# A mixer layer in split fp32: later splits in the first pair, branches one after the other, last chunks bank by bank

## The chip, the cores and the metric

The kernel runs on one core of a Trainium2 chip. Its time is the device time of one execution in microseconds (us); shown is the median of some runs, and for the trace one profiled execution. The core's engines work through queues of their own, in order: TensorE (PE: matrix products into eight PSUM banks; PEld is its weight load), VectorE (DVE), ScalarE (ACT), GpSimd (POOL) and SyncE (SP), which issues most transfers.

## The reference

One layer over 512 tokens of width 2048. All three branches read the same normalised input, each is gated and projected back to width 2048, and their sum goes through one output product:

```python
h = rms_norm(x, norm_g[l]);  proj = h @ w_in[l]          # 2048 -> 13312, split into 13 parts
ya = (short_conv_mixer(a_b, a_c, a_x, conv_w[l]) * silu(a_z)) @ w_branch_a[l]
yb = (chunk_band_attention(q, k, v, ...) * silu(b_z)) @ w_branch_b[l]     # 8 heads of 128
mkv = rms_norm(mem, mem_norm_g[l]) @ w_mem_kv[l]         # 256 memory tokens; mk gets a norm per head
ym = (memory_attention(mq, mk, mv, ...) * silu(m_z)) @ w_branch_m[l]      # 4 heads
merged = sigmoid(g_a + b0) * ya + sigmoid(g_b + b1) * yb + sigmoid(g_m + b2) * ym
x = x + merged @ w_out[l]
```

## The kernel before

All products but the memory's are done in split precision: an fp32 operand is cut into a rounded part `hi` (a cast on ScalarE) and the rest `lo` (a subtraction on VectorE), and three matmuls (hi hi, hi lo, lo hi) stand for one (`split`, `products`, lines 182 to 205).

The wide products go in pairs of 512 columns (`pair`, line 235) by Strassen's scheme: tokens and rows, and columns, are halved, and seven products in the order P1, P5, P6, P3, P7, P2, P4 take the place of eight. Each has four chunks (256 rows of the halved weight, two banks, 12 matmuls), so a pair is 28 steps. A chunk needs its weight block or a difference of two (`raw`, one subtraction on VectorE) split into `whi` and `wlo`. The left operands are blocks of the tokens, A11, S1, S2, S4, S3, A12, A22 (line 233: which product takes which), built once by `Blocks` from four quarters: s1, s2, s4 and s3 are the sums and differences, and a name such as S4 is the split of one, each in two halves (0 and 1) of four rows each. `H` are the blocks of the normalised input, `M` those of the merged branches. A pair ends each product with an evacuation on VectorE (P1 on ScalarE).

The order is written out: a list of steps, each with loads (issued 6 steps ahead), the subtractions, the split of the weights of two steps later, the matmuls, what follows them (`post`), what a table puts at that step (`at_step`), what was put off by some steps (`after`) and tasks taken from a list with a budget per step (`run_steps`, line 123). Each engine keeps that order.

The steps: 16 for memory's keys and values (`kv_steps`, fp32 without a split, meanwhile x is normalised and turned), then the pairs q, k, v, cx, bz, mqz, az, six pairs of gates (beside them the attention's heads), then the branches' products (`branch`, line 798: slabs of four banks and 24 matmuls a step, two steps for a and m, four for b), which add into `mg`, and at last two output pairs o0 and o1 (`out_pair`). The turn of `mg` into the blocks of M is `m_turn`. Memory's head norm is `heads_out` with the name mk: squares on ScalarE, `rstd_of` (line 158: v, a power on GpSimd, then t and r on VectorE), a scaling and a turn. The tiles of the 512-wide intermediate results come from one pool of nine cells (`cel`), gates and x among them; split weights from three buffers each (`wst`).

Of the kernel before, what the change touches and what calls it, by code (L numbers as in the profile page):

```python
# [14 lines left out]
ALU = mybir.AluOpType  # L15
# [13 lines left out]
KB = 2  # L29
# [36 lines left out]
def trunk_layer(ctx: ExitStack, tc, x, mem, gx, gm, w_in, w_kv, bg, cw, hg, relz, w_a, w_b, w_m, w_o, out):  # L66
# [50 lines left out]
    def at_step(i, fn):  # L117
        at.setdefault(i, []).append(fn)
# [78 lines left out]
    def products(banks, w, acts, first, last, cont=False):  # L197

        whi, wlo = w
        for kk in range(KB):  # L200
            for t, ps in enumerate(banks):
                hi, lo = acts(kk, t)
                for i, (l, r) in enumerate(((hi, whi), (hi, wlo), (lo, whi))):
                    PE.matmul(ps, l, r[:, kk, :], start=first and kk == 0 and i == 0,
                              stop=last and kk == KB - 1 and i == 2, skip_group_check=cont)
# [26 lines left out]
    ORDER = ("P1", "P5", "P6", "P3", "P7", "P2", "P4")  # L232
    LEFT = {"P1": "A11", "P5": "S1", "P6": "S2", "P3": "S4", "P7": "S3", "P2": "A12", "P4": "A22"}

    def pair(name, left, w, done, bias=None):


        n = NK // 2 // KB
# [8 lines left out]
        def sub(dst, a, b, c):  # L247
            return lambda: DVE.tensor_tensor(raw[dst, c], raw[a, c], raw[b, c], op=ALU.subtract)
# [69 lines left out]
        for c in range(n):  # L318
            steps[s0 + c].loads.append(loader("11", 0, 0, c))
            steps[s0 + 1 + c].loads.append(loader("12", 0, 1, c))  # L320
            steps[s0 + 7 + c].loads.append(loader("22", 1, 1, c))
            steps[s0 + 19 + c].loads.append(loader("21", 1, 0, c))
            steps[s0 + c].adds.append(sub("11", "12", "11", c))
            steps[s0 + 5 + c].adds.append(sub("11", "22", "11", c))
            steps[s0 + (10, 12, 14, 16)[c]].adds.append(sub("12", "22", "12", c))
            steps[s0 + (20, 21, 22, 24)[c]].adds.append(sub("21", "21", "11", c))
        if bias is not None:
            def load_bias():
                st8["bias"] = bias()
            at_step(s0 - 2, load_bias)  # L330
# [74 lines left out]
    def kv_steps():  # L405
        st = {"ps": {}}
        for c in range(NK // KB):
            for half in range(2):
                def do_load(c=c, half=half):
                    st["raw", c, half] = load(w_kv[c * KB * P:(c + 1) * KB * P, half * S:(half + 1) * S], f"kv{half}_{c}")  # L410

                def mm(c=c, half=half):
                    if c == 0:
                        st["ps"][half] = [bank(f"ps_kv{half}_{t}") for t in range(NMT)]
                    for k in range(c * KB, (c + 1) * KB):
                        for t, ps in enumerate(st["ps"][half]):
                            PE.matmul(ps, mT[k // 8][:, k % 8, t * P:(t + 1) * P], st["raw", c, half][:, k % KB, :],
                                      start=k == 0, stop=k == NK - 1)

                s = Step(mm)  # L420
                s.loads.append(do_load)
                if c == NK // KB - 1:
                    def post(half=half):
                        cells = []
                        for t in range(NMT):
                            kv = cell(f"kv{half}_{t}")
                            ACT.mul(kv, st["ps"][half][t], rm[t])
                            cells.append(kv)
# [22 lines left out]
    class Blocks:  # L451


        def __init__(self, pre, slots, place):
            self.pre, self.slots, self.place, self.at, self.part = pre, slots, place, {}, {}

        def f(self, key, i):
            if key == (1, 1):
# [18 lines left out]
        def do(self, what, i):  # L477
            if what == "s1":
                self.combine("S12", (0, 1), (1, 1), ALU.add, i)
            elif what == "s2":  # L480
                self.combine("S12", "S12", (0, 0), ALU.subtract, i)
            elif what == "s4":
                self.combine("S4", (1, 0), "S12", ALU.subtract, i)
            elif what == "s3":
                self.combine((0, 1), (0, 0), (0, 1), ALU.subtract, i)
            else:
                key = {"A11": (0, 0), "S1": "S12", "S2": "S12", "S4": "S4", "S3": (0, 1), "A12": (1, 0), "A22": (1, 1)}
                self.split(what, i, key[what])

        def left(self, b):  # L490
# [23 lines left out]
        at_step(b + 2, lambda t=t: [x_turn(t, 2), x_turn(t, 3)])  # L514
    for i in range(2):
        for n, what in ((5 + i, "A11"), (7 + i, "A12"), (9, "s1"), (9, "s3"), (10, "S3"), (11, "S1"), (12, "s2"),
                        (12, "s4"), (13 + i, "S4"), (15 + i, "S2"), (17 + i, "A22")):
            at_step(n, lambda i=i, what=what: H.do(what, i))

    def w_pair(src, c0, c1=None):  # L520
# [277 lines left out]
    def branch(br, n, src, nk, names, first, end):  # L798
# [14 lines left out]
        def done(t, ps):  # L813
# [7 lines left out]
            if end is not None:  # L821
# [94 lines left out]
```

## Time and profile before

| what | us |
|---|---|
| median of three runs | 1515.0 (1514.83 to 1516.69) |
| the profiled execution | 1515.63, its span 1513.8 |
| TensorE busy | 1486.6, 98% of the span |
| VectorE busy | 1148.2, 76% |
| ScalarE busy | 706.7, 47% |
| granted TensorE clock, mean | 0.999 |

The span goes from the first to the last instruction of the trace. Busy shares are means over stages. Matmuls overlap their neighbours, so a single one shows 0.39 us where 48 in a row take 10.88. In a row of the timeline the brackets hold how long the engine was idle before, and what ended that.

### The profile page before, as it was taken

How to read it: one execution, taken by the hardware profiler on the slowest of the kernel's cores; microseconds unless marked ns; L12 is line 12 of the kernel's file. 1: busy time of each engine (PE TensorE's matmuls, PEld its weight loads, DVE VectorE, ACT ScalarE, POOL GpSimd, SP SyncE). 2: the span in 40 equal slices, each digit the busy share in tenths (PEclk: the TensorE clock that was granted, in tenths of full speed). 3: DMA queues.
4: the chain of work that ended last, by engine and by line, in shares of the span. 5: the costliest groups of instructions: out<-in, count | busy, mean ns of one | idle time of the engine just before them, and what ended most of it. 6: DMA issues, size and time to landing. Idle time of an engine off the chain costs nothing.

```text
span 1513.8 us, 17882 instructions
## 1 busy us (share of the span) xinstructions
PE 1486.6 (98%) x6696; PEld 1201.1 (79%) x6696; DVE 1148.2 (76%) x1393; ACT 706.7 (47%) x1102; POOL 22.0 (1%) x23
## 2 busy tenths in 40 slices
PE   8989999999999999999999999999999999998998
PEld 4468888788888888888888888888887888886786
DVE  3887778777888878887777778787887545579987
ACT  3565667543444465444444444444445333445442
POOL 0000000000000000000000000000000000000000
PEclk9999999999999999999999999999999999999999
DMA  9524354363326253625446362544735656510724
GB/s 325 190 70 141 135 171 143 92 223 111 119 91 208 70 195 88 201 94 206 134 156 220 106 227 88 186 141 133 254 133 203 207 183 195 201 43 21 256 78 132
DMA packets 139046, 233.45 MB, mean 154 GB/s; under 512 B 9808, under 2 KB 35408, under 8 KB 138320
## 3 DMA queue, kind: packets, MB, share of 16 engines
q1 hardware_dynamic: 130320, 215.54, 43.2%
q10 hardware_dynamic: 8640, 16.78, 3.4%
q8 instruction: 52, 0.85, 0.2%
q14 instruction: 34, 0.28, 0.1%
HBM read 198.73 MB, written 36.17 MB: 155 GB/s over the span
## 4 chain that ended last, share of the span: by engine, by line
PE 85%; DVE 9%; ACT 2%; issue 1%; DMA 1%; POOL 1%; SPq 0%; DVEq 0%; POOLq 0%; ACTq 0%
PE ps_wb L48 6%; PE psY_gb L48 4%; PE psY_ga L48 4%; PE psY_gm L48 3%; PE psY_o L48 3%; PE psZ_gm L48 3%; PE psZ_gb L48 3%; PE ps_wa L48 3%; PE ps_wm L48 3%; PE psZ_ga L48 3%; PE psY_k L48 2%; PE psY_cx L48 2%; PE psY_mqz L48 2%; PE psY_bz L48 2%; PE psY_q L48 2%; PE psY_az L48 2%
## 5 line engine op out<-in xcount | busy, mean ns | idle before, releaser
L48 ACT CAST whi_o_P<-raw_o 128x1024 fp32r<-128x1024 f32 x56 | 58.7, 1053 | 85.7 <-DVE raw_o L48 21.0
L48 DVE TENSOR_TENSOR wlo_gb_P<-raw_gb,whi_gb_P 128x1024 fp32r<-128x1024 f32 x56 | 68.1, 1222 | 31.4 <-ACT whi_gb_P L48 31.3
L48 DVE TENSOR_TENSOR wlo_ga_P<-raw_ga,whi_ga_P 128x1024 fp32r<-128x1024 f32 x56 | 68.2, 1223 | 31.0 <-ACT whi_ga_P L48 30.6
L48 DVE TENSOR_TENSOR wlo_gm_P<-raw_gm,whi_gm_P 128x1024 fp32r<-128x1024 f32 x56 | 68.5, 1223 | 22.8 <-ACT whi_gm_P L48 22.8
L48 DVE TENSOR_TENSOR wlo_o_P<-raw_o,whi_o_P 128x1024 fp32r<-128x1024 f32 x56 | 68.3, 1222 | 20.1 <-ACT whi_o_P L48 15.7
L48 ACT ACTIVATE p<-p,nm 128x128 f32<-128x128 f32 (+3 forms) x32 | 18.0, 564 | 108.4 <-DVE nm L48 100.9
L48 ACT CAST whi_gm_P<-raw_gm 128x1024 fp32r<-128x1024 f32 x56 | 58.8, 1051 | 20.4 <-PE psV_gm L48 5.2
L48 ACT CAST whi_ga_P<-raw_ga 128x1024 fp32r<-128x1024 f32 x56 | 58.1, 1049 | 10.8 <-PE psY_az L48 2.8
L48 ACT CAST whi_gb_P<-raw_gb 128x1024 fp32r<-128x1024 f32 x56 | 58.4, 1049 | 6.9 <-PE psY_gb L48 2.3
L48 ACT COPY p<-ptp 128x256 f32<-128x256 f32 (+3 forms) x48 | 19.6, 409 | 88.3 <-PE ptp L48 88.3
L48 PE MATMUL ps_kv<-raw_kv,mT 128*128 128x512 f32 x128 | 58.7, 612 | 0.3 <-DMA raw_kv<-in_w_kv 0.3
L48 PE MATMUL ps_wb<-whi_wb,yb_hi 128*128 128x512 f32 x128 | 49.8, 389 | 0.0
L48 PE MATMUL ps_wb<-whi_wb,yb_lo 128*128 128x512 f32 x128 | 49.8, 389 | 0.0
L48 PE MATMUL ps_wb<-wlo_wb,yb_hi 128*128 128x512 f32 x128 | 49.8, 389 | 0.0
L48 ACT CAST whi_cx_P<-raw_cx 128x1024 fp32r<-128x1024 f32 x28 | 29.6, 1056 | 42.9 <-PE psY_cx L48 13.2
L48 DVE TENSOR_TENSOR wlo_cx_P<-raw_cx,whi_cx_P 128x1024 fp32r<-128x1024 f32 x28 | 34.3, 1224 | 17.6 <-ACT whi_cx_P L48 15.9
L48 PEld LDWEIGHTS ps_kv<-raw_kv,mT 128*128 128x128 f32 x128 | 24.5, 197 | 28.4 <-issue 27.9
L48 DVE TENSOR_TENSOR wlo_mqz_P<-raw_mqz,whi_mqz_P 128x1024 fp32r<-128x1024 f32 x28 | 34.3, 1223 | 14.2 <-ACT whi_mqz_P L48 12.7
L48 DVE TENSOR_TENSOR wlo_v_P<-raw_v,whi_v_P 128x1024 fp32r<-128x1024 f32 x28 | 34.1, 1222 | 14.0 <-ACT whi_v_P L48 13.8
L48 ACT CAST whi_mqz_P<-raw_mqz 128x1024 fp32r<-128x1024 f32 x28 | 29.4, 1051 | 31.4 <-PE psZ_mqz L48 10.0
L48 ACT CAST whi_bz_P<-raw_bz 128x1024 fp32r<-128x1024 f32 x28 | 29.5, 1054 | 30.8 <-PE psZ_bz L48 7.7
L48 DVE TENSOR_TENSOR wlo_q_P<-raw_q,whi_q_P 128x1024 fp32r<-128x1024 f32 x28 | 34.2, 1223 | 12.5 <-ACT whi_q_P L48 12.3
(661 smaller groups left out, 4675.3 us busy)
## 6 DMA issues: line engine op xcount, KB each, us to landing
raw_ga<-in_w_in SPq DMA_DIRECT2D x32, 512.0 KB, 4.6
raw_gb<-in_w_in SPq DMA_DIRECT2D x32, 512.0 KB, 5.3
raw_gm<-in_w_in SPq DMA_DIRECT2D x32, 512.0 KB, 5.1
raw_o<-in_w_o SPq DMA_DIRECT2D x32, 512.0 KB, 6.8
raw_kv<-in_w_kv SPq DMA_DIRECT2D x16, 512.0 KB, 8.0
raw_q<-in_w_in SPq DMA_DIRECT2D x16, 512.0 KB, 4.4
raw_k<-in_w_in SPq DMA_DIRECT2D x16, 512.0 KB, 4.7
raw_v<-in_w_in SPq DMA_DIRECT2D x16, 512.0 KB, 4.5
```

The source lines that it names most:

```text
L48: ins = getattr(self.engine, op)(*args, **kwargs)
```

## The change

Four things:

- The first pair. The splits of the tokens' blocks S2, S4 and A22 move from steps 13 to 18 to steps 17 to 30 (the q pair begins at step 16), and mk's head norm begins seven steps later.
- The branches go one after the other, all four slabs of a, then of m, then of b, in place of a, m, b for each 512 columns. For that `M` uses other slots: s3 and S3 are done before the output pair instead of in it, and s1, s2, s4, S1, S2 are spread otherwise over its first steps.
- In the last chunk of every product (`last`) the matmuls go bank by bank, all of bank 0's before bank 1's, in place of row block by row block.
- In the output pairs x is added into the cells that the last product will be added to, at step 25 (`add_last`), in place of after it; and the last tile of all is stored in two halves, one issued by SyncE and one by ScalarE.

```diff
 def products(banks, w, acts, first, last, cont=False):
-        for kk in range(KB):
-            for t, ps in enumerate(banks):
+        nt = len(banks)
+        for j in range(KB * nt):
+            kk, t = (j % KB, j // KB) if last else (j // nt, j % nt)
...
 def pair(name, left, w, done, bias=None, addend=None):
+        def add_last():
+            for t, e in enumerate(addend()):
+                DVE.tensor_tensor(cs["a"][t], cs["a"][t], e, op=ALU.add)
+        if addend is not None:
+            at_step(s0 + 25, add_last)
...
 kv_steps
-                            heads_out("mk", cells, 0, hg_sb[:, 3:4], lambda t: mk_d[:, :, t * P:(t + 1) * P])
+                            after(7, lambda: heads_out("mk", cells, 0, hg_sb[:, 3:4], ...))
...
 for i in range(2):       # H, the tokens' blocks: step, what
-                        (12, "s4"), (13 + i, "S4"), (15 + i, "S2"), (17 + i, "A22")):
+                        (12, "s4"), (17 + 2 * i, "S2"), (21 + 2 * i, "S4"), (27 + 3 * i, "A22")):
...
-    M = Blocks("m", {..., "S4": (6, 7), "S3": (0, 13), "A12": (11, 1), "A22": (10, 12)}, {...})
+    M = Blocks("m", {..., "S4": (0, 1), "S3": (6, 7), "A12": (13, 10), "A22": (11, 12)}, {..., "S3": 10, ...})
...
     for n in range(4):
         branch("a", n, w_a, 4, ("ya",), True, None)
+    for n in range(4):
         branch("m", n, w_m, HM, ("ym",), False, None)
+    for n in range(4):
         branch("b", n, w_b, HB, ("yb0", "yb1"), False, m_turn)
...
-                       (7, "S4", 0), (8, "S4", 1), (10, "s3", 0), (10, "s3", 1), (11, "S3", 0), (12, "S3", 1),
+    for n, what, i in ((-7, "A11", 0), (-6, "A11", 1), (-5, "s3", 0), (-5, "s3", 1), (-4, "S3", 0), (-4, "S3", 1),
...
 out_pair, done
+                if (half, t0) != (0, 2):
+                    xr = xs.pop((half, t0 + k))
+                    DVE.tensor_tensor(c, c, xr, op=ALU.add)
+                if i == 1 and half == 0 and t0 == 2 and k == 1:
+                    for eng, j in ((SP, 0), (ACT, 1)):
+                        eng.dma_start(out[ts, n0 + j * MEM:n0 + (j + 1) * MEM], c[:, j * MEM:(j + 1) * MEM])
+                else:
+                    SP.dma_start(out[ts, n0:n0 + S], c)
```

VectorE's queue in the q pair before, from the second split of P1 to the fourth. `hS_lo<-hf_S_484` is a half of S2, `hS_lo<-hf_S_539` one of S4; `raw` is a subtraction of weight blocks, `wlo_q_P_n` the split of a product's chunk n, and v_mk to r_mk is the head norm:

```order
L48 TENSOR_TENSOR wlo_q_P_1_577<-raw_q_518,whi_q_P_1_576 128x1024
L48 TENSOR_TENSOR hS_lo<-hf_S_484,hS_hi 128x1024
L48 TENSOR_TENSOR raw_q_489<-raw_q_516,raw_q_489 128x1024
L48 TENSOR_TENSOR wlo_q_P_2_598<-raw_q_532,whi_q_P_2_597 128x1024
L48 TENSOR_TENSOR hS_lo<-hf_S_484,hS_hi 128x1024
L48 TENSOR_SCALAR v_mk_617<-ss_mk_571 128x8
L48 TENSOR_TENSOR t_mk_621<-r_mk_619 128x8
L48 TENSOR_TENSOR t_mk_621<-t_mk_621,v_mk_617 128x8
L48 TENSOR_SCALAR t_mk_621<-t_mk_621 128x8
L48 TENSOR_TENSOR r_mk_619<-r_mk_619,t_mk_621 128x8
L48 TENSOR_TENSOR raw_q_518<-raw_q_530,raw_q_518 128x1024
L48 TENSOR_TENSOR wlo_q_P_3_630<-raw_q_545,whi_q_P_3_629 128x1024
```

The same queue after, from the split of P6's chunk 1 to that of P6's chunk 2 (`pf` is the evacuation of the second product, P5):

```order
L48 TENSOR_TENSOR raw_q_532<-raw_q_640,raw_q_532 128x1024
L48 TENSOR_TENSOR wlo_q_P_1_734<-raw_q_518,whi_q_P_1_733 128x1024
L48 TENSOR_TENSOR pf_q_749<-psZ_q_671,pa_q_659 128x512
L48 TENSOR_TENSOR pf_q_750<-psZ_q_672,pa_q_660 128x512
L48 TENSOR_TENSOR hS_lo<-hf_S_539,hS_hi 128x1024
L48 TENSOR_SCALAR v_mk_755<-ss_mk_706 128x8
L48 TENSOR_TENSOR t_mk_759<-r_mk_757 128x8
L48 TENSOR_TENSOR t_mk_759<-t_mk_759,v_mk_755 128x8
L48 TENSOR_SCALAR t_mk_759<-t_mk_759 128x8
L48 TENSOR_TENSOR r_mk_757<-r_mk_757,t_mk_759 128x8
L48 TENSOR_TENSOR raw_q_545<-raw_q_665,raw_q_545 128x1024
L48 TENSOR_TENSOR wlo_q_P_2_766<-raw_q_532,whi_q_P_2_765 128x1024
```

The norm has moved from ahead of P1's last split to ahead of P6's third, six chunks later, where it now stands behind an evacuation and the last half of S4.

VectorE's queue at the start of the first output pair before, from the first subtraction for P5 (chunk 0's `raw`) on; `mf_S` are the sums s1, and `mS_lo` from them the two halves of S1:

```order
L48 TENSOR_TENSOR raw_o_110_10260<-raw_o_120_10300,raw_o_110_10260 128x1024
L48 TENSOR_TENSOR wlo_o_P_2_10490<-raw_o_112_10342,whi_o_P_2_10489 128x1024
L48 TENSOR_TENSOR raw_o_111_10302<-raw_o_121_10340,raw_o_111_10302 128x1024
L48 TENSOR_TENSOR wlo_o_P_3_10535<-raw_o_113_10386,whi_o_P_3_10534 128x1024
L48 TENSOR_TENSOR mf_S_10450<-mf_9544,mf_10213 128x1024
L48 TENSOR_TENSOR mS_lo<-mf_S_10450,mS_hi 128x1024 x2
L48 TENSOR_TENSOR raw_o_112_10342<-raw_o_122_10384,raw_o_112_10342 128x1024
L48 TENSOR_TENSOR wlo_o_P_0_10561<-raw_o_110_10260,whi_o_P_0_10560 128x1024
```

The same place after:

```order
L48 TENSOR_TENSOR raw_o_110_10237<-raw_o_120_10273,raw_o_110_10237 128x1024
L48 TENSOR_TENSOR wlo_o_P_2_10499<-raw_o_112_10318,whi_o_P_2_10498 128x1024
L48 TENSOR_TENSOR mS_lo<-mf_S_10425,mS_hi 128x1024
L48 TENSOR_TENSOR raw_o_111_10275<-raw_o_121_10316,raw_o_111_10275 128x1024
L48 TENSOR_TENSOR wlo_o_P_3_10548<-raw_o_113_10395,whi_o_P_3_10547 128x1024
L48 TENSOR_TENSOR mf_S_10425<-mf_10027,mf_10385 128x1024
L48 TENSOR_TENSOR mS_lo<-mf_S_10425,mS_hi 128x1024
L48 TENSOR_TENSOR raw_o_112_10318<-raw_o_122_10393,raw_o_112_10318 128x1024
L48 TENSOR_TENSOR wlo_o_P_0_10570<-raw_o_110_10237,whi_o_P_0_10569 128x1024
```

S1's halves, which stood side by side behind the second sum, now stand apart, the first two ops earlier and the second right behind its own sum; the first sum is done before this place in both.

Later in the same queue before, from P6's last split (not shown) to the fourth split of P3; `mf_9544<-mf_9531,mf_9544` are the two differences s3 and the `mS_lo` from mf_9544 the two halves of S3:

```order
L48 TENSOR_TENSOR raw_o_120_10300<-raw_o_220_10531,raw_o_120_10300 128x1024
L48 TENSOR_TENSOR wlo_o_P_0_10732<-raw_o_220_10531,whi_o_P_0_10731 128x1024
L48 TENSOR_TENSOR mf_9544<-mf_9531,mf_9544 128x1024 x2
L48 TENSOR_TENSOR wlo_o_P_1_10750<-raw_o_221_10557,whi_o_P_1_10749 128x1024
L48 TENSOR_TENSOR pe_o_10765<-psY_o_0_10694,pa_o_10595 128x512
L48 TENSOR_TENSOR pe_o_10766<-psY_o_1_10695,pa_o_10596 128x512
L48 TENSOR_TENSOR mS_lo<-mf_9544,mS_hi 128x1024
L48 TENSOR_TENSOR raw_o_121_10340<-raw_o_221_10557,raw_o_121_10340 128x1024
L48 TENSOR_TENSOR wlo_o_P_2_10775<-raw_o_222_10576,whi_o_P_2_10774 128x1024
L48 TENSOR_TENSOR mS_lo<-mf_9544,mS_hi 128x1024
L48 TENSOR_TENSOR wlo_o_P_3_10799<-raw_o_223_10601,whi_o_P_3_10798 128x1024
```

After, the same rows stand there without these four ops, which now come in the last branch slabs.

## Rows read from the trace of the kernel before

**Rows 1.** Waits of TensorE: us in total, times, longest.

```profile
PE psX_q L48 <- DVE wlo_q_P L48: 4.4, 3, 3.1
PE psY_o L48 <- DVE wlo_o_P L48: 4.1, 3, 1.5
PE psZ_o L48 <- DVE wlo_o_P L48: 3.8, 3, 1.5
PE ps_wa L48 <- DVE wlo_wa L48: 0.9, 1, 0.9
```

**Rows 2.** Stretches: length, busy PE, PEld, DVE, ACT, POOL; clock, DMA share, GB/s.

```profile
90.90:93.70 2.80, 2.77 (x7) 2.19 (x8) 2.80 (x3) 0.12 (x1) 0.00 (x0) 0.50 0.00 0
1357.00:1385.00 28.00, 22.96 (x96) 17.64 (x96) 28.00 (x26) 12.54 (x13) 0.00 (x0) 1.00 0.00 1
```

**Rows 3.** Timeline of TensorE, q pair: start, length, engine, operation, wait before.

```profile
76.09 0.79 PE L48 MATMUL psX_q<-whi_q_P,hA_hi 128*128 128x512 f32 x1
...
90.93 0.79 PE L48 MATMUL psX_q<-wlo_q_P,hA_hi 128*128 128x512 f32 x1 [3.07 <-DVE wlo_q_P L48]
...
94.86 0.40 PE L48 MATMUL psZ_q<-whi_q_P,hS_hi 128*128 128x512 f32 x1
```

**Rows 4.** Timeline of VectorE in the q pair's first product.

```profile
85.84 0.17 DVE L48 TENSOR_SCALAR v_mk<-ss_mk 128x8 f32<-128x8 f32 x1
87.83 0.17 DVE L48 TENSOR_TENSOR t_mk<-r_mk 128x8 f32<-128x8 f32 x1 [1.82 <-POOL r_mk L48]
...
88.53 1.22 DVE L48 TENSOR_TENSOR raw_q<-raw_q,raw_q 128x1024 f32<-128x1024 f32 x1
89.66 1.22 DVE L48 TENSOR_TENSOR wlo_q_P<-raw_q,whi_q_P 128x1024 fp32r<-128x1024 f32 x1
```

**Rows 5.** Timeline of ScalarE: the copies of the first product.

```profile
94.37 1.28 ACT L48 COPY pa_q<-psX_q 128x512 f32<-128x512 f32 x2 [3.35 <-PE psX_q L48]
```

**Rows 6.** Chain that ended last: the second output pair's first product.

```profile
1432.23 10.88 PE psX_o L48 x48
```

**Rows 7.** Timeline of TensorE, first output pair.

```profile
1344.12 0.39 PE L48 MATMUL psX_o<-whi_o_P,mA_hi 128*128 128x512 f32 x1
...
1379.66 0.50 PE L48 MATMUL psY_o<-wlo_o_P,mS_hi 128*128 128x512 f32 x1 [1.14 <-DVE wlo_o_P L48]
```

**Rows 8.** Timeline of VectorE, last branch slab and first output pair.

```profile
1339.96 1.23 DVE L48 TENSOR_TENSOR wlo_o_P<-raw_o,whi_o_P 128x1024 fp32r<-128x1024 f32 x1 [3.08 <-ACT whi_o_P L48]
1342.28 0.69 DVE L48 TENSOR_TENSOR g_b<-ps_wb,g_b 128x512 f32<-128x512 f32 x1 [1.09 <-PE ps_wb L48]
...
1347.59 1.22 DVE L48 TENSOR_TENSOR raw_o<-raw_o,raw_o 128x1024 f32<-128x1024 f32 x1
...
1352.14 1.22 DVE L48 TENSOR_TENSOR mf_S<-mf,mf 128x1024 f32<-128x1024 f32 x1
1353.27 2.43 DVE L48 TENSOR_TENSOR mS_lo<-mf_S,mS_hi 128x1024 fp32r<-128x1024 f32 x2
...
1384.06 2.36 DVE L48 TENSOR_TENSOR mf<-mf,mf 128x1024 f32<-128x1024 f32 x2
...
1388.66 1.22 DVE L48 TENSOR_TENSOR mS_lo<-mf,mS_hi 128x1024 fp32r<-128x1024 f32 x1
```

**Rows 9.** Timeline of ScalarE: the cast of the second half of S1.

```profile
1353.39 1.06 ACT L48 CAST mS_hi<-mf_S 128x1024 fp32r<-128x1024 f32 x1 [1.97 <-DVE mf_S L48]
```

**Rows 10.** Timeline of the end: VectorE, and SyncE's queue (SPq).

```profile
1507.75 1.37 DVE L48 TENSOR_TENSOR pa_o<-psY_o,pa_o 128x512 f32<-128x512 f32 x2 [4.61 <-PE psY_o L48]
1509.04 1.28 DVE L48 TENSOR_TENSOR pa_o<-pa_o,xr 128x512 f32<-128x512 f32 x2
1509.75 0.94 SPq L48 DMA_DIRECT2D out_y<-pa_o  x2
```

**Rows 11.** Issues of transfers: KB each, median us to landing.

```profile
g_a<-g_da SPq DMA_DIRECT2D x16, 256.0 KB, 7.2
...
out_y<-pa_o SPq DMA_DIRECT2D x4, 256.0 KB, 2.5
```

More of the change, by code (lines that the diff above doesn't have):

```diff
@@ L199, in products @@
         whi, wlo = w
-        for kk in range(KB):
-            for t, ps in enumerate(banks):
[L202 to L205, printed above, removed]
+        nt = len(banks)
+        for j in range(KB * nt):
+            kk, t = (j % KB, j // KB) if last else (j // nt, j % nt)
+            hi, lo = acts(kk, t)
+            for i, (l, r) in enumerate(((hi, whi), (hi, wlo), (lo, whi))):
+                PE.matmul(banks[t], l, r[:, kk, :], start=first and kk == 0 and i == 0,
+                          stop=last and kk == KB - 1 and i == 2, skip_group_check=cont)
     def slab(name, src, nk, act, nt, done):
@@ L233, in trunk_layer, with pair @@
     LEFT = {"P1": "A11", "P5": "S1", "P6": "S2", "P3": "S4", "P7": "S3", "P2": "A12", "P4": "A22"}
-    def pair(name, left, w, done, bias=None):
+    def pair(name, left, w, done, bias=None, addend=None):
         n = NK // 2 // KB
@@ L431, in post @@
                         if not half:
-                            heads_out("mk", cells, 0, hg_sb[:, 3:4], lambda t: mk_d[:, :, t * P:(t + 1) * P])
+                            after(7, lambda: heads_out("mk", cells, 0, hg_sb[:, 3:4],
+                                                   lambda t: mk_d[:, :, t * P:(t + 1) * P]))
                     s.post.append(post)
@@ L455, in __init__ @@
             self.pre, self.slots, self.place, self.at, self.part = pre, slots, place, {}, {}
+            self.s3 = "S3" if "S3" in place else (0, 1)
         def f(self, key, i):
@@ L484, in do @@
             elif what == "s3":
-                self.combine((0, 1), (0, 0), (0, 1), ALU.subtract, i)
+                self.combine(self.s3, (0, 0), (0, 1), ALU.subtract, i)
             else:
-                key = {"A11": (0, 0), "S1": "S12", "S2": "S12", "S4": "S4", "S3": (0, 1), "A12": (1, 0), "A22": (1, 1)}
+                key = {"A11": (0, 0), "S1": "S12", "S2": "S12", "S4": "S4", "S3": self.s3, "A12": (1, 0), "A22": (1, 1)}
                 self.split(what, i, key[what])
@@ L826, in branch @@
         at_step(len(steps) - 2, sigmoid)
-    M = Blocks("m", {"A11": (8, 9), "S1": (2, 3), "S2": (4, 5), "S4": (6, 7), "S3": (0, 13), "A12": (11, 1),
-                     "A22": (10, 12)}, {(0, 0): 0, (0, 1): 1, (1, 0): 10, "S12": 11, "S4": 12})
+    M = Blocks("m", {"A11": (8, 9), "S1": (2, 3), "S2": (4, 5), "S4": (0, 1), "S3": (6, 7), "A12": (13, 10),
+                     "A22": (11, 12)}, {(0, 0): 0, (0, 1): 1, (1, 0): 11, "S3": 10, "S12": 10, "S4": 12})
     def m_turn(n, t):
@@ L840, in trunk_layer @@
         branch("a", n, w_a, 4, ("ya",), True, None)
+    for n in range(4):
         branch("m", n, w_m, HM, ("ym",), False, None)
+    for n in range(4):
         branch("b", n, w_b, HB, ("yb0", "yb1"), False, m_turn)
     n_o = len(steps)
-    for n, what, i in ((-7, "A11", 0), (-6, "A11", 1), (-2, "s1", 0), (1, "s1", 1), (1, "S1", 0), (1, "S1", 1),
[2 rows of a table removed]
+    for n, what, i in ((-7, "A11", 0), (-6, "A11", 1), (-5, "s3", 0), (-5, "s3", 1), (-4, "S3", 0), (-4, "S3", 1),
[2 rows of a table added]
                        (14, "A12", 0), (15, "A12", 1), (18, "A22", 0), (19, "A22", 1)):
@@ L854, in done @@
         def done(half, t0, cells):
-            ns = slice((2 * i + half) * S, (2 * i + half + 1) * S)
             for k, c in enumerate(cells):
                 ts = slice((t0 + k) * P, (t0 + k + 1) * P)
-                xr = xs.pop((half, t0 + k))
-                DVE.tensor_tensor(c, c, xr, op=ALU.add)
-                SP.dma_start(out[ts, ns], c)
+                n0 = (2 * i + half) * S
+                if (half, t0) != (0, 2):
[6 more added lines that the diff above has]
+                    SP.dma_start(out[ts, n0:n0 + S], c)
         def get_x(half, t0):
@@ L868, in out_pair @@
         s0 = len(steps)
-        pair(f"o{i}", M.left, w_pair(w_o, 2 * S * i), done)
+        pair(f"o{i}", M.left, w_pair(w_o, 2 * S * i), done, addend=lambda: [xs.pop((0, t)) for t in (2, 3)])
         for n, args in ((15, (1, 0)), (19, (1, 2)), (23, (0, 0)), (27, (0, 2))):
```

3 rows, old and new, of the table n_o are left out of this document.

## The prediction

> **What bounds the kernel now.** I read the page's head first: TensorE is busy 98% of the span at a granted clock of 0.999, so a change of order can only win back the time in which TensorE waits. Then the waits of TensorE [rows 1]: nearly all stand in two places, the first token pair (psX_q) and the first output pair (psY_o, psZ_o), and each waits for a `wlo` split of VectorE. The wait list holds only idle time, so I took the real loss from starts. In the q pair the first product (4 chunks, 48 matmuls) runs from 76.09 to 94.86 = 18.8 us [rows 3]; 48 matmuls without a wait take 10.9 [rows 6], so 7.9 us are lost. The longest wait is 3.07, and behind it 2.8 us run at a granted clock of 0.50, the 1.2 GHz level [rows 2, 3]. The first output pair runs from 1344.12 to 1432.23 = 88.1 us [rows 6, 7]; 28 chunks of 2.72 and 1.75 of transposes make 77.9, so 10.2 are lost. From 1357 to 1385 VectorE is busy 28.0 of 28.0 us, with the memory queues empty [rows 2]: that stretch goes at VectorE's pace. Last, 6.0 us lie between the start of the last two evacuations and the end of the span, 1513.8 [rows 10]. So 7.9 + 10.2 and a part of 6.0 can be had at most.
>
> **The q pair.** Every op that moves here is a 1024-wide one of VectorE (1.22 busy, 1.13 from start to start [rows 4]) with its cast on ScalarE (1.05 [rows 9]). Before, four S4/S2 halves and the mk norm stand among the first product's own splits; the mk norm blocks VectorE from 85.84 to 88.53, 2.7 us, since the op behind it waits 1.82 for GpSimd [rows 4]. After, the first three chunks' splits have at most one subtraction between them, and each arrives before its chunk. So the first product's 7.9 goes. What is late next? I walk VectorE's new queue. TensorE starts at 76.1, its first matmul takes 0.4 longer than usual [rows 3], so the first product ends at 87.4. ScalarE then copies psX (its second copy can begin only now: 0.6 [rows 5]) and makes the second S2 half's cast, which VectorE's `hS_lo` waits for: it starts at 89.2. From there the queue is full: nine ops to the second P6 split, 9 x 1.13 = 10.2, at 99.4; two evacuations 1.2, 100.6; an S4 half 1.1, 101.7; the mk norm 2.7, 104.4; a subtraction and the third P6 split 2.35, 106.8. TensorE wants that split at its eleventh chunk's second matmul, 76.5 + 10 x 2.72 + 0.2 = 103.9. So the mk norm costs 2.9 us there. The clock: a wait of 3.07 was followed by 2.8 us at half speed, the shorter waits of the output pair left it at 1.00 [rows 2, 7]; 2.9 is nearest to 3.07, so I add 1.4 (bounds 0 and 1.4). New loss 4.3, gain 7.9 - 4.3 = 3.6. From the fourth product on each chunk holds two or three VectorE ops at most in 2.72 us, and the two A22 halves, due only at chunk 24, hide in that. Bounds of this term: 0 (the norm costs as much as all before) and 7.9 (all hidden).
>
> **The first output pair.** Bank by bank, bank 0 of the last branch slab is done 18 matmuls (4.1 us) before the slab's end instead of 9. The eight evacuation ops started at 1342.28 and took 5.3 [rows 8]; now they can follow the split that ends at 1341.1 and end at 1346.4, 1.2 earlier. But the second S1 half moves apart from the first: its subtraction ended at 1353.36 and its cast started at 1353.39 [rows 8, 9]. Before, VectorE did the first half's `mS_lo` meanwhile; now that is done already and VectorE waits for the cast, 1.2. Up to the third split of P6 the queue holds 29 ops in both orders: 27 x 1.135 + 1.2 for two evacuations = 31.9, and 1346.4 + 1.2 + 31.9 = 1379.5 against 1347.59 + 31.9 = 1379.5 before [rows 8]. So I expect nothing up to there: TensorE still resumes at about 1379.7 [rows 7] and starts P3 at 1384.9. The stalls only change places (walking the queue, P5's four chunks wait 1.0, 1.8, 0.7 and 1.8). Behind that the four S3 ops (two subtractions from 1384.06, two `mS_lo`, the first at 1388.66 [rows 8]) are gone, 4 x 1.13 = 4.5, moved into the last branch slab, where VectorE is idle 3.08 before one split alone [rows 8]. TensorE's later loss before was 1432.23 - 1384.9 - 16 x 2.72 = 3.8. With 4.5 less work each later split is ahead, the tightest (third of P7, third of P2) within 0.4. I take 3.8 - 0.3 = 3.5. Bounds: 2.0 (the wait for the cast comes through once more), 10.2 (all).
>
> **The branches.** a, m and b slabs have the same matmuls and the same VectorE ops in another order; only the gate loads move. TensorE's one wait there, 0.9, stands before the first slab and stays [rows 1]. With two slabs of gates in flight in 9 cells a load (7.2 us median [rows 11]) still lands about 10 us after the start of the slab before, which takes 10.9. I take 0.
>
> **Bank by bank elsewhere.** It moves no op on VectorE and changes no matmul's cost: before, three matmuls in a row went to one bank, now six. I take 0.
>
> **The tail.** Before: two evacuations from 1507.75, two additions of x to 1510.3, two stores from 1509.75, the end at 1513.8 [rows 10]. After, x is already in, bank 0 is done 1.4 us before the end, and only bank 1's evacuation (0.7) follows the last matmul: it starts where the second did, 1508.4 (1507.75 and 0.7 on), and ends at 1509.1, 1.2 earlier. The additions now stand ahead of the next pair's splits, hidden in a stretch where VectorE is not full. A store of 256 KB lands 2.5 after its issue [rows 11]; of a store in two halves no row tells, between 0 and 1.2 saved; I take 0, since what is halved is only moving the bytes. The Trainium skill, DMA: Bandwidth & Descriptors, section "Issuing engines are not separate DMA queues", speaks against that edit: DMAs started by different engines run on the same 16 DMA engines, and only issue time is saved. By it the term is 0, by a halved landing the whole sum would be 1.2 more; no run here shows a split store yet.
>
> **Sum.** 3.6 + 3.5 + 1.2 = 8.3. The profiled execution took 1515.63 (span 1513.8 and 1.8 around it), 0.6 above the median of the runs shown, 1515.0. So 1507.3 beside the profiled one, 1506.7 beside the median.
>
> **Rivals.**
> First, the mk norm is covered after all: VectorE's queue runs 3 us ahead by then, and the q pair loses nothing. For it: one wait for the psX copy anchors my whole walk. Against it: nine ops of 1.13 in a row hold no slack to win. Then 7.9 + 3.5 + 1.2 = 12.6: 1502.4.
> Second, the q pair gains nothing: with a second split late among P5's (each has about 1 us to spare by my walk) and another stretch at half clock, the 7.9 comes back. Then 3.5 + 1.2: 1510.3.
> Third, the output pair gains nothing: S2 and S4 are now packed a chunk closer to P5, and should VectorE also wait for a cast there, all that S3 gave is eaten. Then 3.6 + 1.2: 1510.2.
> Fourth, slower: gates starve the branches. Four a slabs in a row take four gates each, and a slab's gates can be loaded only into cells that the slab two before has left. Casts for later chunks stand behind the sigmoid on ScalarE. If a load took 17 us instead of 7.2, the sigmoid would be some 7 us late, a chunk's cast with it, and TensorE would lose about 2 us at each of 7 slab changes: 14 us, 1515.0 - 8.3 + 14 = 1520.7. It decides from 12 us a load. For it: a and m slabs double the gates' rate; against it: a median of 7.2.
>
> **How the numbers follow.** Forecast 0.58 at 1506.7; first rival 0.16; second 0.11; third 0.10; fourth 0.05. 0.2% (3 us) is about what a measurement of this kernel tells from no change, so faster means under 1512.0. Faster: all but the fourth and a tenth of the rest, 0.87; same 0.08; slower 0.05. The range goes from 1502.6 (just above the first rival) to 1511.0 (the second and third with some noise).
>
> **What would show it.** The first product of q without a wait, and one wait of some 3 us for `wlo_q_P` near 104 with VectorE's mk ops ahead of it and a lower clock behind it. In the output pair waits in P5 and the third chunk of P6, none over 0.5 from P3 on, and its length 84 to 85 us. One `mS_lo` that waits 1.2 for its cast. At the end the last matmul to the end of the span 1.2 less. Wrong would be: waits on TensorE between the a or m slabs, a wait in q's P5, or waits in P7 and P2 of the output pair.

## The result, and the profile after

The changed kernel takes 1507.09 us (median of 6 runs, 1506.5 to 1510.17) where the kernel before takes 1515.21 (6 runs, 1514.83 to 1516.69): a ratio of 0.9949, 95% interval 0.9936 to 0.9962. That is 8.1 us faster, and the interval leaves out 1. The profiled execution took 1506.83, with a span of 1505.0 and a mean clock of 1.000, 8.8 less than the span before.

Where the 8.8 came from is read off the starts of TensorE's products in the two traces. The first pair begins at the same time and the k pair 4.5 earlier. These are the first matmuls of the k pair and of the second output pair before:

```profile
162.10 0.39 PE L48 MATMUL psX_k<-whi_k_P,hA_hi 128*128 128x512 f32 x1
...
1432.07 0.39 PE L48 MATMUL psX_o<-whi_o_P,mA_hi 128*128 128x512 f32 x1
```

And after:

```profile
157.63 0.39 PE L48 MATMUL psX_k<-whi_k_P,hA_hi 128*128 128x512 f32 x1
...
1424.53 0.39 PE L48 MATMUL psX_o<-whi_o_P,mA_hi 128*128 128x512 f32 x1
```

The first output pair begins 4.4 earlier (1344.12 before, 1339.76 after), so from k to the branches' end nothing changed by more than 0.2. It takes 84.8 where it took 88.0, which is 3.2 more. The rest, 1.3, is the end of the program.

First the waits of TensorE after (us in total, times, longest). They answer to [rows 1]:

```profile
PE psZ_o L48 <- DVE wlo_o_P L48: 4.4, 4, 1.7
PE psY_q L48 <- DVE wlo_q_P L48: 2.7, 1, 2.7
...
PE ps_wa L48 <- DVE wlo_wa L48: 0.9, 1, 0.9
PE psY_o L48 <- DVE wlo_o_P L48: 0.7, 1, 0.7
```

psX_q's 4.4 are gone, and a single wait of 2.7 for psY_q (P6) has come. The branches' one wait, 0.9, is as before. The output pair waits 5.1 instead of 7.9. The timeline of TensorE in the first pair answers to [rows 3]:

```profile
76.08 0.80 PE L48 MATMUL psX_q<-whi_q_P,hA_hi 128*128 128x512 f32 x1
...
87.41 0.39 PE L48 MATMUL psZ_q<-whi_q_P,hS_hi 128*128 128x512 f32 x1
...
106.82 0.50 PE L48 MATMUL psY_q<-wlo_q_P,hS_hi 128*128 128x512 f32 x1 [2.71 <-DVE wlo_q_P L48]
```

The first product takes 11.3 in place of 18.8. The new wait ends at 106.82, and VectorE's timeline shows what stands ahead of the split that ends it:

```profile
89.17 1.23 DVE L48 TENSOR_TENSOR hS_lo<-hf_S,hS_hi 128x1024 fp32r<-128x1024 f32 x1 [1.66 <-ACT hS_hi L48]
...
100.59 1.22 DVE L48 TENSOR_TENSOR hS_lo<-hf_S,hS_hi 128x1024 fp32r<-128x1024 f32 x1
101.72 0.17 DVE L48 TENSOR_SCALAR v_mk<-ss_mk 128x8 f32<-128x8 f32 x1
103.72 0.17 DVE L48 TENSOR_TENSOR t_mk<-r_mk 128x8 f32<-128x8 f32 x1 [1.83 <-POOL r_mk L48]
...
105.55 2.48 DVE L48 TENSOR_TENSOR wlo_q_P<-raw_q,whi_q_P 128x1024 fp32r<-128x1024 f32 x2
```

The norm holds VectorE from 101.72 to 104.41, the same 2.7 as in [rows 4], and the split is 2.7 late. Behind [rows 2]'s wait of 3.07 the clock was 0.50. After this one it was not, in this execution. This is the stretch around it (length, busy PE, PEld, DVE, ACT, POOL; clock, DMA share, GB/s):

```profile
104.00:112.00 8.00, 5.29 (x24) 4.30 (x24) 7.16 (x9) 6.24 (x12) 0.00 (x0) 1.00 0.06 9
```

The same kernel run a second time, beside the second group of experiments, has in the same stretch:

```profile
104.00:112.00 8.00, 5.30 (x17) 4.10 (x17) 6.34 (x9) 5.59 (x12) 0.00 (x0) 0.79 0.07 16
```

The wait is the same there (2.70), but the clock fell to its lower level for part of the stretch, 17 matmuls fit where 24 did, and the k pair starts at 159.3 instead of 157.6. So the drop costs 1.6, in some executions: of the 11 runs of this kernel, six lie at 1506.5 to 1507.2 with a clock of 1.000, and five at 1508.2 to 1510.2 with 0.998 to 0.999. The kernel before scatters in the same way: its nine runs beside the second group of experiments go from 1514.8 at a mean clock of 1.000 to 1517.1 at 0.997.

In the first output pair ([rows 7]) TensorE now waits five times, all by P6's third chunk:

```profile
1339.76 0.39 PE L48 MATMUL psX_o<-whi_o_P,mA_hi 128*128 128x512 f32 x1
...
1353.63 0.50 PE L48 MATMUL psZ_o<-wlo_o_P,mS_hi 128*128 128x512 f32 x1 [0.83 <-DVE wlo_o_P L48]
...
1358.29 0.50 PE L48 MATMUL psZ_o<-wlo_o_P,mS_hi 128*128 128x512 f32 x1 [1.65 <-DVE wlo_o_P L48]
...
1361.70 0.50 PE L48 MATMUL psZ_o<-wlo_o_P,mS_hi 128*128 128x512 f32 x1 [0.35 <-DVE wlo_o_P L48]
...
1366.24 0.50 PE L48 MATMUL psZ_o<-wlo_o_P,mS_hi 128*128 128x512 f32 x1 [1.53 <-DVE wlo_o_P L48]
...
1375.38 0.50 PE L48 MATMUL psY_o<-wlo_o_P,mS_hi 128*128 128x512 f32 x1 [0.69 <-DVE wlo_o_P L48]
```

A bracket holds idle time alone. By starts a chunk that waits costs about 0.3 more than its bracket, since the matmuls behind it no longer overlap at once. What the whole pair loses is its length less 28 chunks of 2.72 and 1.77 of transposes: 6.8 in place of 10.0 (the expectations below say 6.7 or 6.9). VectorE's timeline there answers to [rows 8]:

```profile
1336.75 0.68 DVE L48 TENSOR_TENSOR g_b<-ps_wb,g_b 128x512 f32<-128x512 f32 x1
...
1342.06 1.22 DVE L48 TENSOR_TENSOR raw_o<-raw_o,raw_o 128x1024 f32<-128x1024 f32 x1
...
1350.08 1.23 DVE L48 TENSOR_TENSOR mS_lo<-mf_S,mS_hi 128x1024 fp32r<-128x1024 f32 x1 [1.12 <-ACT mS_hi L48]
```

The evacuations end 2.3 after the pair's first matmul, before 3.5. The wait of 1.12 is the one for S1's cast that was forecast. The end ([rows 10]) now reads, for VectorE and the two queues that store (SPq, ACTq):

```profile
1499.52 0.69 DVE L48 TENSOR_TENSOR pa_o<-psY_o,pa_o 128x512 f32<-128x512 f32 x1 [2.72 <-PE psY_o L48]
...
1500.24 1.69 SPq L48 DMA_DIRECT2D out_y<-pa_o  x2
...
1500.88 0.69 DVE L48 TENSOR_TENSOR pa_o<-psY_o,pa_o 128x512 f32<-128x512 f32 x1 [0.67 <-PE psY_o L48]
1501.61 0.38 ACTq L48 DMA_DIRECT2D out_y<-pa_o  x1
```

One evacuation of 0.69 follows the last matmul, and the span ends 4.2 after its start (before: 5.4 after the start of the last one).

### The profile page after: what moved, and what is told of

Read it like the earlier page. It is cut to its first block, busy times and chain, and to the rows that moved or that the text cites. A ratio compares the mean times of both kernels' runs of the same rounds, so it can differ in the third digit from the quotient of the medians.

```text
span 1505.0 us, 17896 instructions
## 1 busy us (share of the span) xinstructions
PE 1483.8 (99%) x6696; PEld 1200.1 (80%) x6696; DVE 1146.7 (76%) x1393; ACT 707.4 (47%) x1102; POOL 22.0 (1%) x23
## 4 chain that ended last, share of the span: by engine, by line
PE 90%; DVE 6%; ACT 1%; DMA 1%; issue 1%; POOL 0%; SPq 0%; DVEq 0%; ACTq 0%; POOLq 0%
PE ps_wb L48 6%; PE psY_gb L48 4%; PE psY_ga L48 4%; PE psY_o L48 4%; PE psY_gm L48 3%; PE ps_kv L48 3%; PE psZ_gm L48 3%; PE psZ_gb L48 3%; PE ps_wa L48 3%; PE ps_wm L48 3%; PE psZ_ga L48 3%; PE psY_k L48 2%; PE psY_cx L48 2%; PE psZ_o L48 2%; PE psY_mqz L48 2%; PE psY_bz L48 2%
## 5 line engine op out<-in xcount | busy, mean ns | idle before, releaser
L48 DVE TENSOR_TENSOR wlo_wb<-raw_wb,whi_wb 128x1024 fp32r<-128x1024 f32 x16 | 19.6, 1223 | 38.6 <-ACT whi_wb L48 38.6
```

What stands on the lines that cost most here:

```text
L48: ins = getattr(self.engine, op)(*args, **kwargs)
```

## The experiments

They ran on three chips, so each is set against the kernel before on its own chip (1515.88, 1515.74 and 1515.68 us). Against that the changed kernel is 0.9949 and, run again beside the second group, 0.9946; 0.001 is 1.5 us. It did not run beside the first and the third group, and each ratio is good to some 0.0013, so differences of 1 or 2 us are read from the traces and not from the times.

**Undoing each part.** First, the first pair's two tables as before:

```diff
-  after(7, lambda: heads_out("mk", ...))
+  heads_out("mk", ...)
-  (17 + 2 * i, "S2"), (21 + 2 * i, "S4"), (27 + 3 * i, "A22")
+  (13 + i, "S4"), (15 + i, "S2"), (17 + i, "A22")
```

> The changed kernel with the first pair's table and the head norm as before. If the terms are separate, as the traces say (7.4 us lost in q's first product against 2.7 to 3.0 at P6): 4.5 us slower than the changed kernel, 1511.6, with the waits of psX_q back (some 4.9 in the list) and the 2.7 of psY_q gone. Rival, that what is won in q is lost again in k or v where the tasks pile up: less than 2 us slower. The changed kernel's slower executions (1508.5 and 1510.2, at clocks of 0.999 and 0.998) would come from the 2.7 us wait, behind which the clock falls in some executions and not in others; here that wait is replaced by one of 3.1, so all executions should lie at 0.999 and within 1 us.

Measured: 1511.08 us, 0.9968 (0.9956 to 0.9979). The stretch of the first product shows the old loss and the lower clock again:

```profile
87.00:98.00 11.00, 7.92 (x23) 5.97 (x22) 9.75 (x12) 6.57 (x14) 0.46 (x1) 0.69 0.00 0
```

P5 starts 19.7 after the first matmul (changed: 11.3), and the k pair at 163.3. The part is worth 2.9 to 3.3 by the ratios, less than the 4.5 forecast; in the two traces the q pair is 6.0 longer, but the profiled execution is the slowest of the six here. The runs also scatter over 2.3 us and not 1: two of the six have a mean clock of 1.000, which suggests that this longer wait (3.08 in the trace) does not lower the clock every time either.

Second, the branches' order with its blocks:

```diff
-  "S4": (0, 1), "S3": (6, 7), "A12": (13, 10), "A22": (11, 12)     (one loop over n for each branch, s3 and S3 at -5 and -4)
+  "S4": (6, 7), "S3": (0, 13), "A12": (11, 1), "A22": (10, 12)     (one loop over n for a, m, b, s3 and S3 at 10 to 12, the rest of the table as before)
```

> The changed kernel with the branches interleaved and the merged blocks' table and slots as before. The first output pair lost 10.2 before and 6.9 after. By the walk of VectorE's queue the evacuation bank by bank starts that queue 1.2 us earlier and the new place of S1 gives it away again; so undoing the order alone leaves the 1.2: 3.3 - 1.2 = 2.1 slower, 1509.2, and no wait in P5's second chunk. Rival, that the order of the branches is what lets the evacuation be early: the full 3.3, 1510.4. Second rival, that the branches' order itself costs something (gates loaded into cells just left): then less than 1 slower.

Measured: 1510.52 us, 0.9964 (0.9951 to 0.9976). The output pair starts at 1339.8 as in the changed kernel, so the order of the branches itself costs and gives nothing; the pair is 2.7 longer, between the 2.1 forecast and the rival's 3.3. VectorE waits for one cast there too, a shorter one:

```profile
1346.22 1.23 DVE L48 TENSOR_TENSOR wlo_o_P<-raw_o,whi_o_P 128x1024 fp32r<-128x1024 f32 x1 [0.61 <-ACT whi_o_P L48]
```

Third, the last chunks in the old order:

```diff
-  kk, t = (j % KB, j // KB) if last else (j // nt, j % nt)
+  kk, t = (j // nt, j % nt)
```

> The changed kernel with the last chunks row block by row block again. VectorE's queue at the output pair starts 1.2 us later, so 1.2 us slower there; at the tail bank 0 is done 0.7 instead of 1.4 us before the end, which still covers its evacuation: 0. In all 1508.3. Rival, that six matmuls in a row to one bank cost or save time by themselves over some 110 last chunks: 0.01 us each would be 1 us either way. Second rival: nothing, since the pair's P5 waits for the S1 cast anyway: 1507.1.

Measured: 1509.44 us, 0.9956 (0.9943 to 0.997). The first output pair is 1.3 longer (forecast 1.2), and VectorE's evacuations wait for the last slab again:

```profile
1339.12 0.69 DVE L48 TENSOR_TENSOR g_b<-ps_wb,g_b 128x512 f32<-128x512 f32 x1 [1.09 <-PE ps_wb L48]
```

From the k pair to the output pair it takes 1182.1, as the changed kernel does, so six matmuls in a row to one bank cost and save nothing. The span ends 4.3 after the last evacuation's start (changed: 4.2), so the bank order is worth 0.1 at the end. In P5 a wait of 2.00 stands here, and the clock falls behind it:

```profile
1356.01 0.50 PE L48 MATMUL psZ_o<-wlo_o_P,mS_hi 128*128 128x512 f32 x1 [2.00 <-DVE wlo_o_P L48]
```

```profile
1357.00:1361.00 4.00, 3.95 (x10) 2.59 (x9) 3.97 (x5) 1.99 (x2) 0.00 (x0) 0.57 0.00 0
```

That fall costs the pair little: its later waits in P5 and P6 end 1.2 after those of the changed kernel, counted from the pair's start, like the first.

Fourth, the additions and the store at the end:

```diff
-  if (half, t0) != (0, 2): ...          (x added ahead of the last product; the last tile stored in halves)
+  xr = xs.pop((half, t0 + k)); DVE.tensor_tensor(c, c, xr, op=ALU.add); SP.dma_start(out[ts, n0:n0 + S], c)
```

> The changed kernel with x added after the last product and the last tile stored in one piece. From the last matmul to the end of the span it took 5.4 before and 4.1 after; the additions are two ops of 0.6 behind the last evacuation, and the half store may give 0.1. So 1.2 to 1.3 slower, 1508.3, all behind the last matmul. Rival, that bank by bank gave most of it (bank 0's evacuation off the end): 0.6 or less.

Measured: 1509.67 us, 0.9955 (0.9943 to 0.9968). The span ends 5.4 after the last evacuation's start (changed: 4.2), so this part is worth 1.3, as forecast. The pair o0 is as in the changed kernel. The four parts, by ratios against 0.9949, sum to 0.0047, 7.1 us, and against 0.9946 to 8.9: the whole, within the intervals.

**The store alone.** The additions stay ahead, the last tile goes in one piece:

```diff
-  if i == 1 and half == 0 and t0 == 2 and k == 1:
+  if False:
```

> The changed kernel, but the last tile of the output is stored in one piece of 256 KB by SyncE's queue, not in two of 128 KB by two queues. Forecast: nothing (0 to 0.3 slower), so the tail's 1.3 us are the addition moved ahead and the order bank by bank. Rival (half a store lands sooner): the end comes 0.5 to 1.2 later than in the changed kernel.

Measured: 1508.15 us, 0.9952 (0.994 to 0.9965). The last evacuation starts at 1504.51 and the span ends at 1508.6: 4.1, against 4.2 with two halves. The split store gives nothing; the end's gain is the additions, and 0.1 of the bank order.

**The norm alone.** It goes back into the first product, the blocks' new table stays:

```diff
-  after(7, lambda: heads_out("mk", ...))
+  heads_out("mk", ...)
```

> The changed kernel, but the norm of memory's heads stands where it did before (right behind the chunk that gives it, among the splits of the first product); the token blocks' second half stays at its new steps. Theory (seven operations of VectorE and ScalarE stood among the first product's splits before, and each takes its own 1.13 from them, the norm 2.7): alone, the norm makes TensorE wait some 2 to 2.7 in the first product, and the 2.7 at the third chunk of P6 goes: the same time as the changed kernel, -0.3 +- 1. Rival (the norm's wait for GpSimd made nearly all of the old loss, the blocks nothing): the first product loses 6 to 7.5 again and the time is 3 to 4 above the changed kernel, near the kernel with both edits undone (0.9968 of before).

Measured: 1506.2 us, 0.9937 (0.9924 to 0.9949). On TensorE two small waits stand in the first and second product, and none at P6:

```profile
85.86 0.50 PE L48 MATMUL psX_q<-wlo_q_P,hA_hi 128*128 128x512 f32 x1 [1.35 <-DVE wlo_q_P L48]
...
89.26 0.50 PE L48 MATMUL psZ_q<-wlo_q_P,hS_hi 128*128 128x512 f32 x1 [0.39 <-DVE wlo_q_P L48]
```

The q pair takes 80.9 to the k pair's start (changed: 81.6 at full clock, 83.2 where it fell), so 0.7 less at full clock; by the ratios it is 1.4 to 1.8, where -0.3 +- 1 was forecast. The first product takes 13.0 here (before 18.8, changed 11.3). So most of what cured it is the blocks' table. Moving the norm by seven steps gave nothing on the whole: it made one longer wait out of two short ones, and the clock fell behind the longer one in some executions. The norm moved with the blocks in their old places was not run.

**The norm behind more products.**

```diff
-  after(7, ...heads_out("mk"...));   (21 + 2 * i, "S4"), (27 + 3 * i, "A22")
+  after(10, ...heads_out("mk"...));  (21 + 4 * i, "S4"), (29 + 4 * i, "A22")
```

> The changed kernel as it is, run again as the reference for the three that run beside it. Expected ratio to the kernel before: 0.995, as measured first (0.9949). If the 2.7 us wait at the third chunk of P6 in the first pair lowers the granted clock in some executions alone, its runs scatter over 3 us (1506.5 to 1510 before), the slower ones with a clock of 0.998 to 0.999.

> The changed kernel, but in the first pair the two S4 halves are cast and split at steps 21 and 25 (not 21 and 23), the two A22 halves at steps 29 and 33 (not 27 and 30), and the norm of memory's heads is three steps later, behind the products that the first pair still lacks. Theory (the norm's 2.7 us on VectorE stand ahead of P6's third split, so TensorE waits 2.7 there): the wait goes to 0.3 or less, psX_k starts 2.4 to 2.7 earlier, and 1.4 to 1.6 more in executions whose clock fell behind the wait: 2.7 us faster than the changed kernel, and less scatter, every clock 1.00. Rival (VectorE is full up to that chunk and the wait is the queue's, not the norm's): the wait comes back a chunk or two later at the same size, 0 +- 0.5.

Measured side by side: the changed kernel 1508.23, 0.9946 (0.9934 to 0.9958); this one 1505.02, 0.9928 (0.9914 to 0.9942), with every clock at 1.000 and runs within 0.9 us (the changed kernel: 2.0). The wait at P6 is gone, and the k pair starts at 155.0, 2.6 earlier than in the execution at full clock and 4.2 earlier than in the one beside it. By medians it gains 3.2 (forecast 2.7). But set against the changed kernel's execution at full clock its span is only 1.4 shorter; most of the rest is the clock. Its waits show where some of it went:

```profile
PE psY_v L48 <- DVE wlo_v_P L48: 1.3, 3, 0.7
PE psY_k L48 <- DVE wlo_k_P L48: 1.1, 2, 0.6
```

Those were 0.3 and 0.6. The k and v pairs take 163.2 together in place of 162.0, so 1.2 comes back there; what follows the norm (memory's heads are turned on TensorE) is later too, but which operation it is was not followed.

**S4 later in the output pairs.**

```diff
-  (2, "s4", 0), (4, "s4", 1), (7, "S4", 0), (8, "S4", 1)
+  (9, "s4", 0), (11, "s4", 1), (10, "S4", 0), (12, "S4", 1)      (s1_1, S1_0, S1_1 at 1; s2, S2 at 3 to 6)
```

> The changed kernel, but in the output pairs S4 (its subtractions and its splits) is formed only after both S2 halves: s4 at steps 9 and 11, the S4 halves at 10 and 12 (before: subtractions at 2 and 4, halves at 7 and 8), and both S1 halves in one step. Theory (what TensorE loses in P5 and P6 of the first output pair is VectorE's queue of operations that are not due yet; every operation moved behind a chunk takes 1.13 off what that chunk waits for): four operations leave the queue ahead of P6's third split, the first output pair loses about 2 to 3 us in place of 6.9, so 4 to 4.7 faster than the changed kernel. Rival (the four come back before P3, whose splits they are): P3 waits for them, 0 to 1 faster, with waits of 1 to 2 us at P3's chunks.

Measured: 1506.65 us, 0.994 (0.9927 to 0.9952). The loss of the pair falls from 6.8 to 5.2, 1.6 and not 4 to 4.7. The waits in P5 shrink to one of 0.39 and P6 keeps three of 0.26 to 0.41, but new ones stand in P3 and P7:

```profile
1385.62 0.50 PE L48 MATMUL psZ_o<-whi_o_P,mS_lo 128*128 128x512 f32 x1 [0.63 <-DVE mS_lo L48]
...
1397.10 0.50 PE L48 MATMUL psY_o<-wlo_o_P,mS_hi 128*128 128x512 f32 x1 [0.53 <-DVE wlo_o_P L48]
```

Neither theory's number held. The four operations were not gone but later, and VectorE is busy 10.0 of 10.0 us from 1382 to 1392 in this trace (8.99 in the changed kernel): it has no room there to take them.

**Both.** The two edits together:

```diff
+  (the first pair's table of "The norm behind more products", the output pairs' table of "S4 later")
```

> Both of the two edits beside it: the first pair's S4, A22 and norm spread out, and the output pairs' S4 formed late. Theory: the two places are 1200 us apart and share nothing, so the gains add: 2.7 + 4.4 = 7.1 faster than the changed kernel, about 1500 where the changed kernel takes 1507. Rival: a wait elsewhere or the clock takes part of it back, and the sum is under 5.

Measured: 1503.57 us (4 runs, 1503.29 to 1503.69), 0.9919 (0.9905 to 0.9932). The gains add, 3.2 and 1.6 to 4.7, and each pair takes what it took with its own edit alone (q 78.8, the output pair 83.2). The sum is under 5, the rival's number, but not for its reason: it is below the forecast because S4's gain was. This is the fastest version that computes the layer, 12.2 us under the kernel before.

**S4 left out.** The test of what forming S4 later left open, whether VectorE's pace is the bound at all:

```diff
-  (2, "s4", 0), (4, "s4", 1), (7, "S4", 0), (8, "S4", 1)
-  return self.at[b]
+  return self.at["S2" if b == "S4" and self.pre == "m" else b]
```

> The changed kernel, but the output pairs never form S4: its two subtractions and two splits (four operations of VectorE of 1.13, two casts of ScalarE) are left out, and the fourth product takes S2's cells in its place, so the output's numbers are other ones. Theory (in the first output pair TensorE goes at the pace of VectorE, which is full from the last evacuation to the end of P6 and was only shifted by forming S4 later, since P3 wants it at once): taken out altogether, the four give 4 to 4.7 us, the loss of the first output pair falls from 6.7 to some 2.3. Rival (what sets the pace is something else, as the casts of ScalarE or the waits' own restarts): no more than the 1.6 that forming S4 later gave.

Measured: 1503.72 us, 0.9922 (0.991 to 0.9934). The loss falls from 6.8 to 3.4, twice what forming S4 later gave, 0.6 to 1.3 less than forecast. TensorE's timeline shows the rest:

```profile
1353.36 0.50 PE L48 MATMUL psZ_o<-wlo_o_P,mS_hi 128*128 128x512 f32 x1 [0.83 <-DVE wlo_o_P L48]
...
1356.77 0.50 PE L48 MATMUL psZ_o<-wlo_o_P,mS_hi 128*128 128x512 f32 x1 [0.39 <-DVE wlo_o_P L48]
...
1360.17 0.50 PE L48 MATMUL psZ_o<-wlo_o_P,mS_hi 128*128 128x512 f32 x1 [0.39 <-DVE wlo_o_P L48]
...
1363.58 0.50 PE L48 MATMUL psZ_o<-wlo_o_P,mS_hi 128*128 128x512 f32 x1 [0.39 <-DVE wlo_o_P L48]
```

P5's chunks stand 3.41 apart, that is 3 VectorE operations of 1.135, where 12 matmuls take 2.72. So there TensorE goes at VectorE's pace to the hundredth.

**S4's subtractions on GpSimd**, in the kernel with the norm spread:

```diff
-  DVE.tensor_tensor(self.f(d, i), self.f(a, i), self.f(b, i), op=op)
+  eng = POOL if d == "S4" and self.pre == "m" else DVE
+  eng.tensor_tensor(self.f(d, i), self.f(a, i), self.f(b, i), op=op)
```

> The kernel with the first pair's norm, S4 and A22 spread out (0.9928 of before), and in it S4's two subtractions of the output pairs on GpSimd in place of VectorE. Theory (VectorE's queue sets the pace there): two operations of 1.13 leave it ahead of the third chunk of P6, 2.0 to 2.3 faster, 0.9914 of before; S4's splits are wanted 10 us after the subtractions, enough for GpSimd at up to 4 us each. Rival (a GpSimd operation on as many elements slows VectorE's while it runs): VectorE's operations beside it take longer than their 1.22, and the gain is 0 or less than 0.

Measured: 1507.4 us, 0.9945 (0.9931 to 0.9958), where the same kernel without it was at 0.9928. GpSimd's timeline, and VectorE's beside it:

```profile
1353.41 3.19 POOL L48 TENSOR_TENSOR mf_S<-mf,mf_S 128x1024 f32<-128x1024 f32 x1 [785.10 <-DVE mf_S L48]
1358.96 3.24 POOL L48 TENSOR_TENSOR mf_S<-mf,mf_S 128x1024 f32<-128x1024 f32 x1 [2.36 <-DVE mf_S L48]
```

```profile
1353.15 1.22 DVE L48 TENSOR_TENSOR raw_o<-raw_o,raw_o 128x1024 f32<-128x1024 f32 x1
1354.29 3.39 DVE L48 TENSOR_TENSOR wlo_o_P<-raw_o,whi_o_P 128x1024 fp32r<-128x1024 f32 x1
...
1359.87 3.41 DVE L48 TENSOR_TENSOR wlo_o_P<-raw_o,whi_o_P 128x1024 fp32r<-128x1024 f32 x1
```

The operation that VectorE had begun 0.26 before GpSimd's took its usual 1.22. The next one, each time, took 3.4 and ended 1.1 after GpSimd's: by these times VectorE got on only when GpSimd was through. Two subtractions of 1.13 were taken off VectorE and 2 x 2.2 put on it. TensorE's wait for the first of these splits is 2.55, the clock falls behind it (0.57 from 1357 to 1361), and the pair loses 8.8 (without this edit 6.9). The rival holds. The Trainium skill, GPSIMD Engine Reference, section "Specifications", says that GpSimd shares its SBUF interfaces with VectorE, with contention for VectorE instructions of two SBUF inputs; the trace agrees, and gives the price: 2.2 us for each.

## Why the prediction was right

**The first product, 7.9 us, right.** It takes 11.3, so 7.5 is gone, all but the slower first matmul; the walk itself ends the product at 87.4 and so gives 7.5, yet the sum took 7.9. The cause was left open: the sum charged the norm and the four halves together. With the halves moved, the norm in its old place costs 2.1 by its two waits' starts (1.51 in the first product, 0.55 in the second), so most of the loss came with the halves.

**The new stall, right in place and size.** The walk of VectorE's queue gave the split's end as 106.8 and TensorE's wait as 2.9. The trace has TensorE resume at 106.82, 2.87 late. The anchor (ScalarE's copies of psX, then S2's cast, 89.2) was 89.17. Putting the norm alone back removed the wait, which shows that it is the norm's; spreading it, which moved half of S4 too, removed it as well.

**The clock, 1.4, right in some executions.** The forecast took the drop as sure. In the profiled execution it did not come, so the q pair gave 4.5 and not 3.6; where it came it cost 1.6, and the pair gave 2.8. With five of eleven runs on the lower clock the mean of this term is 0.7. So 3.6 lies between the two gains that an execution can have, and that the sum came so near the median is in part luck.

**The output pair, 3.5 forecast, 3.2 measured.** The waits in P5 were forecast as 1.0, 1.8, 0.7 and 1.8; by starts they are 0.99, 1.81, 0.51 and 1.69. The earlier evacuations are given back by the wait for the cast: P6's third chunk resumes 35.6 after the pair's first matmul, before 35.5, so nothing is gained up to there, as forecast. No wait above 0.1 is left behind P6. The sum took the chain's first row, 1432.23, for the pair's end; its first matmul is at 1432.07, so the loss to be had there was 0.16 less than the 3.8. Taken apart, the two causes do not add: undoing the bank order costs the pair 1.3 and undoing the blocks' order 2.7, together 4.0 for a gain of 3.2. With the early evacuations and the old blocks VectorE waits 0.61 for another cast, a wait that none of the other three has.

**Branches and gate loads, nothing: right.** TensorE's waits there are as before, and a gate of branch a lands in 7.3 us (before 7.2), so the fourth rival never came near its 12 us.

**The tail, 1.2 forecast, 1.3 in the trace.** It is the additions, by the runs above. The store in halves gave nothing, as taken. What the prediction cites of the Trainium skill, DMA: Bandwidth & Descriptors, section "Issuing engines are not separate DMA queues", agrees: the second queue moved the end by no more than 0.1, and not forward.

The sum was 8.3, and 8.1 came out by medians, 8.8 in the profiled execution. The first rival (the norm hidden) is answered by the wait of 2.71, the second and third by the two pairs' gains.

## What to carry to other kernels

Where one engine feeds another through a queue in written order, count its operations between two due splits: at more than 2.72 / 1.135 = 2.4 a chunk it sets the pace, and moving an operation later helps only if the later stretch has idle time. Ask of an operation that waits inside the queue (here 1.8 us for GpSimd) what is due behind it at its new place, and try its old place with the other moves kept (here that was 0.7 us better at full clock). Do not hand large two-operand work from VectorE to GpSimd beside a full VectorE (it cost this kernel 1.9 us in the pair).

## What the runs showed of the hardware

The same wait of 2.7 us lowered TensorE's clock in some executions and left it at 1.00 in others of the same kernel, worth 1.6 us a time; of the eight traces that have it, over all runs, the clock fell at its end or just behind it in five. Waits of 1.66 and less went without a fall in these traces. A fall came with one of 2.00 (bank order undone), one of 2.11 ahead of a transpose of x (the store alone), one of 2.55 (GpSimd) and those of 3.07 and 3.08. And one GpSimd operation on 128x1024 fp32 (3.2 us) held up the VectorE operation issued beside it until it ended, 2.2 us each. Six matmuls in a row into one PSUM bank cost no more than three (1182.1 us from the k pair to the output pair either way).
